# A two-row weight product, taken as raw fp32 instead of as a split pair, at the start of a fused diffusion block

## The chip, the cores and the metric

The kernel runs on one core of one Trainium2 chip. The metric is the device time of one execution in microseconds (us); the lower the better. TensorE (PE) multiplies, VectorE (DVE) and ScalarE (ACT) do elementwise work, GpSimd (POOL) does some of it too, and SyncE (SP) issues most DMA transfers.

## What is computed

One layer of a diffusion backbone over 512 latent tokens and 256 context tokens of width 1024, in fp32. The part that the change touches is the very first: two conditioning vectors, one for the latent tokens and one for the context tokens, go through a SiLU and are multiplied by the modulation weights; the first two of the six blocks of 1024 columns give the shift and the scale of the first normalisation.

```python
silu_c = jax.nn.silu(c)
silu_cc = jax.nn.silu(c_ctx)
mod = silu_c @ w_mod[i] + b_mod[i]
mod_c = silu_cc @ w_mod[i] + b_mod[i]
sh1, sc1, g1, sh2, sc2, g2 = jnp.split(mod, 6, axis=-1)
csh1, csc1, cg1, csh2, csc2, cg2 = jnp.split(mod_c, 6, axis=-1)
h = modulated_norm(x, g_norm1[i], sh1[:, None], sc1[:, None])
hc = modulated_norm(ctx, g_norm1[i], csh1, csc1)
proj = h @ w_in[i]
...
x = x + g1 * mix_stream(...)
x = x + g2 * moe(modulated_norm(x, g_norm2[i], sh2, sc2), ...)
return rmsnorm(x, g_final)
```

After it come the input projection, a bidirectional state-space scan (SSD) with its convolution, a pooling branch, a gated MLP branch, the merge with the output projection, and a mixture of 16 experts.

## The kernel before, in words

Nearly every large product is made of three: each fp32 operand is split into a high part `hi`, rounded to a reduced fp32 form (fp32r), and a rest `lo`, and TensorE multiplies high by high, high by low and low by high (`mm3`, lines 102 to 105). The weights are split as they arrive (`split`, lines 81 to 90): ACT writes `hi` (line 87), DVE or POOL writes `lo` as the difference (line 89).

The first phase (lines 764 to 866) computes shift and scale. Its weights are read as 16 tiles `wraw` of 128 x 1024 fp32 (512 KB), eight for each half `hf` of the columns: a tile holds 128 rows of the weights and 512 columns of the shift beside 512 of the scale. `w_unit` (line 798) loads one tile through a pool of five buffers, splits it, and multiplies `hi` and `lo` by `cs4`, four columns: the high and the low parts of the two conditioning vectors. Each half accumulates over its eight tiles into two PSUM tiles of 4 x 512 (`ptmp` for the first half, `pacc` for the second). A buffer comes free for the load five tiles later when the split has read it.

`rows_to_cols` (line 808) copies the four rows out (DVE line 810, ACT line 811), turns them into columns on TensorE while adding high and low rows with `sel4` (line 815), and makes `sh` and `gs` on DVE (lines 821 to 823). `h_block` (line 825) transposes the normalised tokens (line 830), applies `gs` and `sh` (line 835), and splits the result into `hTh` and `hTl` (lines 837, 838). The first half serves the blocks j = 0 to 3, the second half the blocks 4 to 7.

Behind it, `dt_phase` (line 887) multiplies a small slice of the input weights, turns it into columns (line 901), and runs a chain of small DVE operations (lines 905 to 920) which ends in products on TensorE (lines 924 to 926). `xbc_tile` and `conv_tile` make the inputs of the scan (convolution on DVE, line 970), `z_block` the gate (ACT, line 1168), `ssd_decay` and `ssd_group` the scan; `mix_prep` prepares constants for the later branches (lines 1030, 1032).

The order on each engine is set by a scheduler from the program text and its own costs. Engines take their instructions in that order, so an instruction that waits holds back all that stand behind it on its engine.

Of the kernel before, what the change touches and what calls it, by code (L numbers as in the profile page):

```python
# [7 lines left out]
FT = mybir.dt.float32  # L8
# [3 lines left out]
AF = mybir.ActivationFunctionType  # L12
# [7 lines left out]
KD = 8  # L20
# [18 lines left out]
def dap(t, off, ap):  # L39
    return bass.AP(tensor=t.tensor, offset=t.offset + off, ap=ap)  # L40
# [3 lines left out]
def backbone_kernel(ctx: ExitStack, tc: tile.TileContext, x, c, ctxt, c_ctx, w_mod, b_mod, g_norm1,  # L44
# [4 lines left out]
    V, S, G, T = nc.vector, nc.scalar, nc.gpsimd, nc.tensor  # L49
# [5 lines left out]
    def pool(name, bufs=1, space=None, side="left"):  # L55
        kw = {"space": space} if space else {"reuse_waits": "tile"}
        return tc.tile_pool(name=name, bufs=bufs, **({"side": side} if space is None else {}), **kw)
# [16 lines left out]
    def ptmp(shape=None, dt=FT):  # L74
        return tmp.tile(shape or [128, 512], dt, tag="tmp", name="ptmp")
# [5 lines left out]
    def split(raw, n, after=None):  # L81
        nsplit[0] += 1
        eng = G if lo_eng[0] is None and nsplit[0] % 1000 == 3 else lo_eng[0] or V
        hp_, lp_ = more_hl if more_hl and nsplit[0] % 4 == 0 else (hip, lop)
        hi = hp_.tile([128, 1024], FR, tag="hi", name="hi")
        lo = lp_.tile([128, 1024], FR, tag="lo", name="lo")
        S.activation(hi[:, :n], raw[:, :n], AF.Copy)  # L87
        with tc.issue_after(after.ins) if after else nullcontext():
            eng.tensor_tensor(lo[:, :n], raw[:, :n], hi[:, :n].bitcast(FT), op=OP.subtract)  # L89
        return hi, lo  # L90
# [668 lines left out]
    sck = sc.rearrange("p (q k) -> p k q", q=2)  # L759
    V.tensor_copy(cs4[:, :, 0:2], sck)  # L760
    V.tensor_tensor(cs4[:, :, 2:4], sck, cs4[:, :, 0:2].bitcast(FT), op=OP.subtract)
    sel4 = cst.tile([4, 2], FT)
    V.tensor_tensor(sel4, ident[0:4, 0:2], ident[0:4, 2:4], op=OP.add)
    with ExitStack() as p1:
        xp = p1.enter_context(pool("xp"))
        f1p = p1.enter_context(pool("f1p", 2))
# [7 lines left out]
        def load(dst, src):  # L774

            with tc.issue_after(queue[0].ins) if queue[0] else nullcontext():
                queue[0] = nc.sync.dma_start(dst, src)
# [20 lines left out]
        def w_unit(hf, k, pm):  # L798
            raw = wrp.tile([128, 1024], FT, tag="wraw", name="wraw")
            load(raw.rearrange("p (s n) -> p s n", s=2),  # L800
                 dap(w_mod, k * 128 * 6144 + hf * 512, [[6144, 128], [1024, 2], [1, 512]]))
            hi, lo = split(raw, 1024)
            for s in range(2):
                cs = slice(s * 512, (s + 1) * 512)
                T.matmul(pm[s], lhsT=cs4[:, k], rhs=hi[:, cs], start=k == 0, stop=False)
                T.matmul(pm[s], lhsT=cs4[:, k], rhs=lo[:, cs], start=False, stop=k == KD - 1)

        def rows_to_cols(hf, pm):
            mrow = f1p.tile([4, 2, 512], FT, tag="mrow", name="mrow")
            V.tensor_copy(mrow[:, 0], pm[0])  # L810
            S.activation(mrow[:, 1], pm[1], AF.Copy)
            pv = ptmp([128, 2, 4, 2])
            for s in range(2):
                for j in range(4):
                    T.matmul(pv[:, s, j], lhsT=mrow[:, s, j * 128:(j + 1) * 128], rhs=sel4, start=True, stop=True)
            js = slice(hf * 4, hf * 4 + 4)

            def bc(c0):
                return pcol[:, c0 + hf * 4:c0 + hf * 4 + 4].unsqueeze(2).to_broadcast([128, 4, 2])

            V.tensor_tensor(sh[:, js], pv[:, 0], bc(24), op=OP.add)
            V.tensor_tensor(gs[:, js], pv[:, 1], bsc1[:, js].unsqueeze(2).to_broadcast([128, 4, 2]), op=OP.add)
            V.tensor_tensor(gs[:, js], gs[:, js], bc(16), op=OP.mult)
# [18 lines left out]
        pm = [ptmp([4, 512]) for _ in range(2)]  # L842
        for k in range(KD):
            w_unit(0, k, pm)
            if k == 1:
                norm_x(2, 6)
        pm2 = [pacc([4, 512]) for _ in range(2)]
        w_unit(1, 0, pm2)
        w_unit(1, 1, pm2)
        rows_to_cols(0, pm)  # L850
        w_unit(1, 2, pm2)
        w_unit(1, 3, pm2)
# [3 lines left out]
        load_x(0)  # L856
        load_x(1)
        rows_to_cols(1, pm2)
        norm_x(0, 2)
        for j in range(4):  # L860
# [525 lines left out]
```

## Time and profile before

| | us |
|---|---|
| median of 3 runs (lowest, highest) | 1037.87 (1037.62, 1039.67) |
| the profiled execution, its own time | 1038.74 |
| its span, from the first to the last instruction | 1036.9 |
| PE busy in the span | 946.9 |
| DVE busy | 820.9 |
| ACT busy | 596.9 |
| POOL busy | 189.7 |

The rows further down are quoted from this one profiled execution. Times in them are microseconds from the start of the span; mean durations are in ns where marked. A matmul's end is modelled, so that successive products overlap in the rows.

### The profile page before, as it was taken

What the parts mean: (1) busy time and instruction counts of PE and PEld (TensorE: products, weight loads), DVE (VectorE), ACT (ScalarE), POOL (GpSimd) and SP (SyncE); (2) the same over time, 40 slices, a digit from 0 to 9 for tenths busy, and PEclk for the clock granted to TensorE, in tenths of its full rate; (3) what the DMA queues carried; (4) which work ended last, traced back from release to release, by engine and by line L of the source; (5) the groups of instructions that cost most, each with busy time, mean ns of one, the idle gap of its engine ahead of it and who ended that gap; (6) DMA issues with size and microseconds to landing.
All of it is one profiled execution on the core that took longest, in us unless ns stands there. A gap on an engine that the chain in (4) does not pass through costs nothing.

```text
span 1036.9 us, 13348 instructions
## 1 busy us (share of the span) xinstructions
PE 946.9 (91%) x4598; PEld 769.4 (74%) x4598; DVE 820.9 (79%) x1221; ACT 596.9 (58%) x884; POOL 189.7 (18%) x144
## 2 busy tenths in 40 slices
PE   3897989998898979999999999978999999999964
PEld 0486778886786857888888888867888888888842
DVE  6878976997878996677486434579999999999897
ACT  5665846667556333622332432445788888888843
POOL 2024313114222340000000010331111111111140
PEclk9998999999999989999999999988999999999987
DMA  8832361314223222276576558678999999999322
GB/s 271 280 91 60 119 201 41 116 47 143 61 61 86 64 65 71 82 244 215 172 217 210 162 166 288 257 245 318 326 355 362 361 375 372 375 361 364 107 73 82
DMA packets 100898, 203.92 MB, mean 197 GB/s; under 512 B 9998, under 2 KB 55290, under 8 KB 100827
## 3 DMA queue, kind: packets, MB, share of 16 engines
q1 hardware_dynamic: 95474, 194.19, 54.5%
q0 software_dynamic: 5136, 8.78, 3.6%
q8 instruction: 37, 0.61, 0.2%
q14 instruction: 35, 0.28, 0.1%
q10 hardware_dynamic: 216, 0.07, 0.0%
HBM read 197.25 MB, written 13.71 MB: 203 GB/s over the span
## 4 chain that ended last, share of the span: by engine, by line
PE 64%; DVE 22%; ACT 5%; DMA 4%; issue 3%; ACTq 0%; POOL 0%; SPq 0%; DVEq 0%; POOLq 0%
PE pacc L104 18%; PE pacc L103 18%; PE pacc L105 18%; DVE cv L970 5%; DVE lo L89 2%; PE ptmp L400 1%; DMA wraw<-in_w_mod_dram 1%; DVE w L1132 1%; DMA agb<-agd 1%; PE ptmp L1094 1%; PE ptmp L1096 1%; DVE agb L1126 1%; PE ptmp L423 1%; DVE r L1274 1%; DVE y L1103 1%
## 5 line engine op out<-in xcount | busy, mean ns | idle before, releaser
L87 ACT ACTIVATE hi<-raw 128x1024 fp32r<-128x1024 f32 (+1 forms) x199 | 209.0, 1057 | 168.0 <-PE pacc L104 75.9
L89 DVE TENSOR_TENSOR lo<-raw,hi 128x1024 fp32r<-128x1024 f32 (+1 forms) x165 | 203.6, 1254 | 58.8 <-ACT hi L87 51.7
L103 PE MATMUL pacc<-hTh,hi 128*128 128x512 f32 (+1 forms) x392 | 156.7, 401 | 4.9 <-ACT ytok L1168 3.5
L104 PE MATMUL pacc<-hTl,hi 128*128 128x512 f32 (+1 forms) x392 | 158.0, 403 | 0.0
L105 PE MATMUL pacc<-hTh,lo 128*128 128x512 f32 (+1 forms) x392 | 156.6, 400 | 0.0
L104 PE MATMUL pacc<-lo,xhl 128*128 128x512 f32 x384 | 151.5, 395 | 4.2 <-DVE lo L89 3.9
L103 PE MATMUL pacc<-hi,xhl 128*128 128x512 f32 x384 | 153.1, 402 | 0.0
L105 PE MATMUL pacc<-hi,xhl 128*128 128x512 f32 x384 | 150.5, 393 | 0.0
L89 POOL TENSOR_TENSOR lo<-raw,hi 128x1024 fp32r<-128x1024 f32 x34 | 91.1, 2684 | 197.6 <-ACT hi L87 187.8
L103 PEld LDWEIGHTS pacc<-hTh,hi 128*128 128x128 f32 (+1 forms) x392 | 74.0, 189 | 21.5 <-ACT ytok L1168 3.9
L104 PEld LDWEIGHTS pacc<-lo,xhl 128*128 128x128 f32 x384 | 72.9, 190 | 20.4 <-DVE lo L89 6.1
L970 DVE SCALAR_TENSOR_TENSOR cv<-xr,pcol,cv 128x770 f32<-128x770 f32 (+1 forms) x64 | 70.9, 1108 | 20.9 <-ACT cv L968 20.2
L105 PEld LDWEIGHTS pacc<-hTh,lo 128*128 128x128 f32 (+1 forms) x392 | 73.9, 189 | 16.2 <-issue 1.0
L104 PEld LDWEIGHTS pacc<-hTl,hi 128*128 128x128 f32 (+1 forms) x392 | 74.0, 189 | 16.0 <-issue 1.1
L105 PEld LDWEIGHTS pacc<-hi,xhl 128*128 128x128 f32 x384 | 72.5, 189 | 15.5
L103 PEld LDWEIGHTS pacc<-hi,xhl 128*128 128x128 f32 x384 | 72.9, 190 | 14.6
L142 DVE SCALAR_TENSOR_TENSOR lacc<-raw,sc,lacc 128x1024 f32<-128x1024 f32 x32 | 41.1, 1284 | 29.4 <-DMA raw<-in_w_mod_dram 29.0
L89 DVE TENSOR_TENSOR lo<-r,hi 128x1024 fp32r<-128x1024 f32 x42 | 50.1, 1219 | 4.7 <-PE pacc L104 3.0
L87 ACT ACTIVATE hi<-r 128x1024 fp32r<-128x1024 f32 x42 | 44.0, 1062 | 7.8 <-PE pacc L105 7.2
L480 POOL DMA_INDIRECT xg<-h2d,toki x16 | 19.2, 1201 | 156.8 <-PE ptmp L400 82.5
L1145 PE MATMUL pacc<-lo,hTh 128*128 128x512 f32 x96 | 38.6, 402 | 0.0
L1144 PE MATMUL pacc<-hi,hTh 128*128 128x512 f32 x96 | 38.2, 398 | 0.0
(410 smaller groups left out, 1894.8 us busy)
## 6 DMA issues: line engine op xcount, KB each, us to landing
raw<-in_w_e_in_dram SPq DMA_DIRECT2D x78, 512.0 KB
raw<-in_w_in_dram SPq DMA_DIRECT2D x60, 512.0 KB
raw<-in_w_e_out_dram SPq DMA_DIRECT2D x36, 512.0 KB
raw<-in_w_mod_dram SPq DMA_DIRECT2D x32, 512.0 KB
r<-in_w_e_in_dram SPq DMA_DIRECT2D x28, 512.0 KB
wraw<-in_w_mod_dram SPq DMA_DIRECT2D x16, 512.0 KB
agb<-agd SPq DMA_DIRECT2D x16, 512.0 KB
r<-in_w_e_out_dram SPq DMA_DIRECT2D x14, 512.0 KB
```

The costliest lines, as they stand in the source:

```text
L87: S.activation(hi[:, :n], raw[:, :n], AF.Copy)
L89: eng.tensor_tensor(lo[:, :n], raw[:, :n], hi[:, :n].bitcast(FT), op=OP.subtract)
L103: T.matmul(ps, lhsT=sh, rhs=mh, start=first, stop=False)
L104: T.matmul(ps, lhsT=sh, rhs=ml, start=False, stop=False)
L105: T.matmul(ps, lhsT=sl, rhs=mh, start=False, stop=last)
L142: V.scalar_tensor_tensor(a, raw, sc[:, k:k + 1], a, op0=OP.mult, op1=OP.add)
L400: T.transpose(pt[:, k], xgt[:, (h * 4 + k) * 128:(h * 4 + k + 1) * 128], ident)
L423: T.transpose(pt[:, k], hid[:, k * 128:(k + 1) * 128], ident)
L480: G.indirect_dma_start(out=dst, out_offset=None, in_=h2d[:, :], in_offset=bass.IndirectOffsetOnAxis(ap=idx, axis=0), bounds_check=L - 1, o ...
L970: V.scalar_tensor_tensor(oo, r[:, lo0 + j:lo0 + j + n], wcol(j), oo, op0=OP.mult, op1=OP.add)
L1144: T.matmul(pv[t], lhsT=a, rhs=wh[:, kk], start=k == 0, stop=False)
L1145: T.matmul(pv[t], lhsT=a, rhs=wl[:, kk], start=False, stop=False)
```

## The change

For the first half (`hf == 0`) the tile is no longer split. Its two 512-column parts are multiplied, as the fp32 values that were loaded, by `sck`, the two fp32 columns of the conditioning vectors. `rows_to_cols` then copies two rows instead of four and uses the first two rows of `sel4`, which are an identity. The second half stays as it was.

```diff
@@ w_unit
             load(raw.rearrange("p (s n) -> p s n", s=2),
                  dap(w_mod, k * 128 * 6144 + hf * 512, [[6144, 128], [1024, 2], [1, 512]]))
+            if hf == 0:
+                for s in range(2):
+                    T.matmul(pm[s][0:2], lhsT=sck[:, k], rhs=raw[:, s * 512:(s + 1) * 512],
+                             start=k == 0, stop=k == KD - 1)
+                return
             hi, lo = split(raw, 1024)
@@ rows_to_cols
-            mrow = f1p.tile([4, 2, 512], FT, tag="mrow", name="mrow")
-            V.tensor_copy(mrow[:, 0], pm[0])
-            S.activation(mrow[:, 1], pm[1], AF.Copy)
+            nr = 2 + hf * 2
+            mrow = f1p.tile([4, 2, 512], FT, tag="mrow", name="mrow")[:nr]
+            V.tensor_copy(mrow[:, 0], pm[0][:nr])
+            S.activation(mrow[:, 1], pm[1][:nr], AF.Copy)
...
-                    T.matmul(pv[:, s, j], lhsT=mrow[:, s, j * 128:(j + 1) * 128], rhs=sel4, start=True, stop=True)
+                    T.matmul(pv[:, s, j], lhsT=mrow[:, s, j * 128:(j + 1) * 128], rhs=sel4[:nr], start=True,
+                             stop=True)
```

Lines behind the insertion move down: line 805 of the kernel before is line 810 of the changed one, 815 is 821, 830 is 837, 1168 is 1175. The scheduler also writes the engines' orders anew, as far as the pooling branch; from there on they are the same.

On PE, the end of the first half and the start of the second, before (`sel` is `sel4`, `x` the tokens, `cs` is `cs4`):

```order
L805 MATMUL ptmp<-hi,cs_131 4x512 x2
L806 MATMUL ptmp<-lo,cs_131 4x512 x2
L815 MATMUL ptmp<-sel_134,mrow 128x2 x4
L830 MATMUL ptmp<-ident,x_147 128x128
L830 MATMUL ptmp<-ident,x_151 128x128
L830 MATMUL ptmp<-ident,x_155 128x128
L805 MATMUL pacc<-hi,cs_131 4x512 x2
```

The same place on PE in the changed kernel:

```order
L722 MATMUL ptmp<-ident,crow 128x80
L804 MATMUL ptmp<-wraw,sc 2x512 x16
L810 MATMUL pacc<-hi,cs_131 4x512 x2
L821 MATMUL ptmp<-sel_134,mrow 128x2 x4
L837 MATMUL ptmp<-ident,x_147 128x128
```

The 32 products of split tiles in the first half have become 16 of raw tiles, in one piece.

On SP, the queue of the loads, before (`x` of `in_ctx_dram` is a context token tile, `raw` a tile of the input weights, the first of them for `dt_phase`):

```order
L777 DMA wraw<-in_w_mod_dram 128x2x512 x7
L94 DMA raw<-in_w_in_dram 128x8x32
L777 DMA wraw<-in_w_mod_dram 128x2x512
L94 DMA raw<-in_w_in_dram 128x8x128
L777 DMA wraw<-in_w_mod_dram 128x2x512 x8
L777 DMA x_392<-in_ctx_dram 128x1024
```

The same place on SP in the changed kernel:

```order
L777 DMA wraw<-in_w_mod_dram 128x2x512 x16
L777 DMA x_344<-in_ctx_dram 128x1024
L777 DMA x_348<-in_ctx_dram 128x1024
L94 DMA raw<-in_w_in_dram 128x8x32
L94 DMA raw<-in_w_in_dram 128x8x128 x4
```

The two loads of input weights that stood among the `wraw` loads now stand behind all sixteen of them and behind the context tokens.

On ACT, where the first gate block is read out of PSUM (line 1168) amid the decay weights of the scan, before:

```order
L1168 ACT_TABLE_LOAD
L1168 ACTIVATE ytok<-pacc 128x512
L1125 ACTIVATE w<-agb,nag 128x128 x4
L1131 ACTIVATE w<-cbu,dtt 128x128 x2
L1128 ACT_TABLE_LOAD
L1128 ACTIVATE agb<-agb 128x512
L1168 ACT_TABLE_LOAD
L1168 ACTIVATE ytok<-pacc 128x512 x3
L1030 ACTIVATE wsT<-ptmp 128x512
```

The same place on ACT in the changed kernel:

```order
L1135 ACTIVATE agb<-agb 128x512
L1138 ACTIVATE w<-cbu,dtt 128x128 x2
L1175 ACT_TABLE_LOAD
L1175 ACTIVATE ytok<-pacc 128x512 x4
L1037 ACTIVATE wsT<-ptmp 128x512
```

Two of the three table loads ahead of `wsT` are gone from here; the whole program has 38 of them before and after.

## Rows read from the trace of the kernel before

**Rows 1.** The page: busy time by engine, and the longest chain by engine.

```profile
PE 946.9 (91%) x4598; PEld 769.4 (74%) x4598; DVE 820.9 (79%) x1221; ACT 596.9 (58%) x884; POOL 189.7 (18%) x144
...
PE 64%; DVE 22%; ACT 5%; DMA 4%; issue 3%; ACTq 0%; POOL 0%; SPq 0%; DVEq 0%; POOLq 0%
```

**Rows 2.** Chain of waits, 0 to 120 us: start, length, what ended last.

```profile
9.06 8.89 DMA wraw<-in_w_mod_dram
...
36.39 5.20 DMA wraw<-in_w_mod_dram
...
49.06 1.87 PE ptmp L815 x16
```

**Rows 3.** Timeline of PE, first half: start, length, what [idle before <- releaser].

```profile
15.31 1.01 PE L805 MATMUL ptmp<-hi,cs 128*4 128x512 f32 x2 [5.35 <-ACT hi L87]
...
19.17 1.00 PE L805 MATMUL ptmp<-hi,cs 128*4 128x512 f32 x2
21.78 0.63 PE L806 MATMUL ptmp<-lo,cs 128*4 128x512 f32 x2 [1.62 <-DVE lo L89]
...
28.75 0.62 PE L806 MATMUL ptmp<-lo,cs 128*4 128x512 f32 x2
```

**Rows 4.** Busy time by stretch; behind the engines: granted clock, DMA share, GB/s.

```profile
20.00:23.40 3.40, 1.37 (x5) 0.18 (x4) 2.78 (x3) 3.40 (x5) 0.00 (x0) 1.00 0.82 210
23.40:26.80 3.40, 3.18 (x8) 0.97 (x9) 3.40 (x4) 2.81 (x3) 0.00 (x0) 0.50 1.08 336
```

**Rows 5.** Instructions by tile, tile wraw: durations min/median/max in ns, starts.

```profile
L87 ACT ACTIVATE hi<-wraw x16: 1040/1042/1059, 14.2 to 41.7; 128x1024 fp32r<-128x1024 f32 x16
L89 DVE TENSOR_TENSOR lo<-wraw,hi x16: 1210/1218/1226, 15.3 to 44.8; 128x1024 fp32r<-128x1024 f32 x16
```

**Rows 6.** Timeline of PE, two raw fp32 products, then one, 512 columns each.

```profile
374.12 3.78 PE L1286 MATMUL ptmp<-o,pwt 128*128 128x512 f32 x4 [5.99 <-DVE o L1280]
...
391.42 1.13 PE L1286 MATMUL ptmp<-o,pwt 128*128 128x512 f32 x2 [1.43 <-DVE o L1280]
```

**Rows 7.** Busy time by stretch, at these two places (granted clock third from the end).

```profile
374.00:376.00 2.00, 1.88 (x3) 0.85 (x4) 2.00 (x2) 0.60 (x1) 2.00 (x1) 0.50 0.00 0
391.00:393.00 2.00, 1.35 (x3) 0.49 (x3) 2.00 (x3) 0.42 (x1) 0.00 (x0) 1.00 0.00 0
```

**Rows 8.** Timeline of SP, its DMA issues.

```profile
23.59 13.16 SPq L777 DMA_DIRECT2D wraw<-in_w_mod_dram  x8
```

**Rows 9.** Waits of the SP queue, 0 to 60 us: total, times, longest.

```profile
SPq L777 <- DVE lo L89: 15.6, 11, 2.9
```

**Rows 10.** Timeline of DVE, 29 to 50 us.

```profile
29.18 0.68 DVE L810 COPY mrow<-ptmp 4x512 f32<-4x512 f32 x1 [1.07 <-PE ptmp L806]
...
32.92 0.17 DVE L821 TENSOR_TENSOR sh<-ptmp,pcol 128x8 f32<-128x8 f32 x1 [0.96 <-PE ptmp L815]
...
34.42 0.80 DVE L835 TENSOR_SCALAR f<-ptmp,gs,sh 128x512 f32<-128x512 f32 x1
...
36.28 0.68 DVE L838 TENSOR_TENSOR hTl<-f,hTh 128x512 fp32r<-128x512 f32 x1
...
47.49 0.68 DVE L810 COPY mrow<-pacc 4x512 f32<-4x512 f32 x1 [0.56 <-PE pacc L806]
```

**Rows 11.** Waits of PE, 45 to 100 us: total, times, longest.

```profile
PE ptmp L924 <- DVE inv L1046: 5.4, 1, 5.4
```

**Rows 12.** Timeline of ACT, then of PE, at the first gate block.

```profile
129.50 1.28 ACT L1128 ACT_TABLE_LOAD   x1
...
132.03 1.28 ACT L1168 ACT_TABLE_LOAD   x1
...
135.44 1.13 PE L1032 MATMUL ptmp<-wsT,ones 128*128 128x512 f32 x2 [0.56 <-ACT wsT L1030]
```

**Rows 13.** Busy time by stretch, the scan and what follows the pooling branch.

```profile
92.00:360.00 268.00, 248.28 (x1286) 208.30 (x1286) 221.73 (x409) 161.76 (x310) 78.76 (x45) 0.98 0.32 95
...
400.00:660.00 260.00, 259.92 (x1186) 213.66 (x1184) 154.61 (x179) 93.28 (x130) 11.72 (x16) 1.00 0.61 198
```

## The prediction

> **What bounds the kernel now.** I read the page first: PE is busy for 91% of the span, and 64% of the longest chain runs through it [rows 1]. Then the busy times by stretch: between 400 and 660 us PE is busy 259.92 of 260 us [rows 13], and there its order is the same before and after. So whatever the change gains or loses up to the pooling branch is carried to the end, and the question is when PE gets through the first 400 us.
>
> The chain of waits shows what sets the pace at the start: the loads of the `wraw` tiles, first plainly (8.89 us), then again for the last tile, whose load is issued at 36.39 and ends 5.20 us later; after it come the products that turn the second half's rows into columns, at 49.06 [rows 2]. The loads are late because they wait for buffers: SP stood 15.6 us in all, eleven times, until DVE had written a `lo` [rows 9]. Five buffers stand against sixteen loads, and the first load of the second half was issued at 23.59 [rows 8]. The reader is to see here that the split holds the buffers. What the change gives PE in return, and whether the buffers come free earlier, is then the matter.
>
> **The cost of one raw product.** The timeline has raw fp32 products of 512 columns at another place: each shows as two records. Two products took 3.78 us at a granted clock of 0.50, one took 1.13 us at 1.00 [rows 6, 7]. With a record p long at full clock, 2p long at half, and a drain d: 8p + d = 3.78 and 2p + d = 1.13, so p = 0.44 and d = 0.25. [...] Those products had 128 weight columns and these have two. I take the same price: four weight columns in the first half and 128 elsewhere pay alike for fp32r products of 512 columns.
>
> **The first half.** Before, the first tile is there at 14.2, when its split starts [rows 5]; PE starts at 15.31 and ends at 28.75 + 0.62 = 29.4 [rows 3]. PE's work there is only 32 products; it waits for splits. In the changed kernel PE starts at 14.2 and has 8 x 1.77 = 14.1 us of work at full clock, 8 x 3.53 = 28.3 at half. The clock: pairs of products took 1.01 and 1.00 at the start and 0.63 from 21.78 [rows 3], so it ran at the half level until some 5 us after the first product; later a thin stretch (1.37 us busy of 3.40) was followed by one at 0.50 [rows 4]. I take 5 us at half, then full: 5 / 3.53 = 1.42 tiles, then 6.58 x 1.77 = 11.6, so the first half ends at 14.2 + 5 + 11.6 + 0.2 = 31.0, that is **+1.6**. Bounds: full throughout, 28.5 (-0.9); half throughout, 42.7 (+13.3).
>
> [...]
>
> The removed 8 splits (1.04 us each on ACT, 1.22 on DVE [rows 5]) cost nothing now that could be won directly: they lie beside the loads, and DVE has nothing else to do until the first half is done. Their gain is the buffers. With the clock as above, the fourth tile is done at 23.8, and the first load of the second half goes out at 24.0 against 23.59 [rows 8]: **no gain**, since PE now holds a buffer about as long as the split did.
>
> **The second half.** Now DVE sets the pace. Behind the copy of the rows (before at 29.18, in the change at 31.0) it has to do 0.65 + 8 `lo` at 1.17 (back to back) + 4 `f` at 0.72 + 3 `hTl` at 0.62 + 0.4 of small ones + a wait of 0.96 for the columns [rows 5, 10] = 16.1 us, so the last `lo` ends at 47.1 and the copy of the second half's rows starts near 47.7, against 47.49 [rows 10]. Before, DVE was as late, because it waited for loads between. The last load goes out when the third `lo` is written, 6.2 us behind the first half: 37.2 against 36.39 [rows 2], and lands at 42.4, before DVE wants it.
>
> Moved with it: the small load for `dt_phase` now stands behind the sixteen tiles and two context tiles, two of 1.6 us each (512 KB at 336 GB/s [rows 4]) and about 1 us of its own after the last of them, near 46.5; its first two products stand ahead of the columns' products on PE, so these start at 48 to 49.5, against 49.06 [rows 2]. **0 for the phase** (from -2.3 to +1.5, by the first half's end and this load). Ahead of line 901 PE then has five products of 512 columns more to do and seven of 256 fewer. A wide one costs about 0.22 us (an estimate: 260 us over 1186 products [rows 13]), a narrow one half: +0.3.
>
> **Behind it.** Ahead of line 924, for which PE waited 5.4 us [rows 11], the new order has 73 products of 512 columns where there were 82. If the DVE chain to line 924 is as long, that wait grows by 9 x 0.22 = 2.0 and the work comes later. From 92 to 360 us PE is idle for 19.7 of 268 us [rows 13], so other waits may cover it: 0 to +2.0, taken as **+1.0**. At the first gate block two table loads of 1.28 us leave the way to `wsT`, for which PE waited [rows 12]: -2.6 to 0 there; but they come back later on ACT: 0 to +2.6. Taken as **-1.3**. Other small moves in the scan I set at nothing, with their cover the same idle time.
>
> Sum: 0 + 0.3 + 1.0 - 1.3 = 0. The profiled execution took 1038.74, 0.87 above the median of the runs; against the median, I forecast **1037.9**, no change. A measurement of this kernel can tell about 0.2%, 2.1 us, from no change.
>
> **Rivals.**
>
> *Faster.* The clock rises early, the first half ends at 28.5, and DVE's 16.1 us start 2.5 us sooner than I take it, so that the copy starts at 45.2, 2.3 ahead of 47.49; the table loads at the gate are won and not paid again. For it: DVE and ACT are idle until the first half ends, and ACT waits often in the scan. Against it: the dt load still stands ahead of the columns' products. -2.3 - 2.6 + 0.3 + 0.5 = -4.1: 1033.8.
>
> *Slower, one mechanism: the clock stays at half* under raw products with two columns. The half ends at 42.7, DVE's work behind it begins 11.7 us later than in my sum, and no load is left to hide it: 1049.6. Each us at half beyond my 5 costs 0.5, so it decides once the clock stays down for some 9. Against it: with four columns the clock did rise [rows 3]; nothing in the trace shows two.
>
> *Slower, the order.* PE's 2.0 us behind line 924 aren't covered, and the table loads come back where ACT is waited for: 0.3 + 2.0 - 2.6 + 2.6 + 1.5 (late dt load) = +3.8: 1041.7.
>
> *The change doesn't do what it says:* raw tiles free buffers no sooner than split ones. That is my sum.
>
> **How the numbers follow.** No change 0.37 (1035.8 to 1040); faster rival 0.30; order rival 0.22; half clock 0.08; 0.03 for more gain in the scan than I can see. So faster 0.33, same 0.37, slower 0.30. The range takes in the ends of the two middle rivals with their bounds and leaves out the half clock: 1031.5 to 1043.5.
>
> **What would show it.** Right: 32 records on line 804, about 0.44 long at full clock; the last of them near 31; SP waiting for PE, not DVE, for loads 6 to 13; the copy of the second half's rows near 47.7; PE's wait at line 931 (924 before) longer than 5.4; one table load less ahead of the gate's rows. Wrong: a granted clock of 0.50 through the 20s; records of half that length; the columns of the second half more than 1.5 us from 49; or a scan whose end moves by more than 3 us against the end of the first phase.

## The result, and the profile after

The changed kernel takes 1045.69 us (median of 9 runs, 1040.98 to 1050.12) against 1037.87 (9 runs, 1035.34 to 1039.67): a ratio of 1.0076, interval 1.0055 to 1.0097. It is slower. The profiled execution took 1047.23 with a span of 1045.5, 8.6 more than the span of before.

The engines' shares hardly change [rows 1], and the first half does what it should. The page (busy time, and the longest chain by engine), then PE's busy time by stretch (granted clock third from the end), then the tile view (min/median/max in ns):

```profile
PE 958.2 (92%) x4598; PEld 774.5 (74%) x4598; DVE 808.3 (77%) x1213; ACT 589.5 (56%) x876; POOL 186.9 (18%) x144
...
PE 66%; DVE 21%; ACT 5%; DMA 4%; issue 2%; POOL 0%; ACTq 0%; SPq 0%; DVEq 0%; POOLq 0%
```

```profile
18.50:30.40 11.90, 11.90 (x29) 2.30 (x28) 0.88 (x2) 1.66 (x3) 0.00 (x0) 1.00 0.84 265
```

```profile
L804 PE MATMUL ptmp<-wraw,sc x32: 592/592/1057, 14.4 to 29.8; 128*2 128x512 f32 x32
```

The 32 records start at 14.42; from 18.6 on they follow each other every 0.43 us, before that every 0.85, and the last ends at 30.3. From 18.5 PE is busy without a gap (11.90 of 11.90 us) at a granted clock of 1.00. SP now waits for PE where it waited for DVE [rows 9], and the copy of the second half's rows starts where it did [rows 10]. SP's waits from 0 to 60 us (total, times, longest), then DVE's timeline:

```profile
SPq L777 <- PE ptmp L804: 12.9, 8, 3.7
SPq L777 <- DVE lo L89: 5.2, 3, 4.0
```

```profile
47.70 0.67 DVE L816 COPY mrow<-pacc 4x512 f32<-4x512 f32 x1
```

The loss begins behind it. PE's timeline before and after, from 43 us (start, length, [idle before <- releaser]); L815 and L821 are the columns, L103 to L105 with 512 columns are wide products of `dt_phase` and of the scan's first tile:

```profile
43.63 0.47 PE L103 MATMUL pacc<-hTh,hi 128*32 128x512 f32 x1 [1.37 <-ACT hi L87]
...
45.60 0.63 PE L104 MATMUL pacc<-hTl,hi 128*32 128x512 f32 x1
46.03 0.63 PE L103 MATMUL pacc<-hTh,hi 128*128 128x512 f32 x1
46.45 0.63 PE L104 MATMUL pacc<-hTl,hi 128*128 128x512 f32 x1
...
47.52 0.40 PE L105 MATMUL pacc<-hTh,lo 128*32 128x512 f32 x1
...
48.99 1.94 PE L815 MATMUL ptmp<-sel,mrow 4*128 4x2 f32 x16
```

```profile
44.13 0.62 PE L811 MATMUL pacc<-lo,cs 128*4 128x512 f32 x2 [1.37 <-DVE lo L89]
44.60 0.62 PE L810 MATMUL pacc<-hi,cs 128*4 128x512 f32 x2
46.88 1.02 PE L811 MATMUL pacc<-lo,cs 128*4 128x512 f32 x2 [1.66 <-DVE lo L89]
47.70 0.63 PE L103 MATMUL pacc<-hTh,hi 128*32 128x512 f32 x1
48.12 0.63 PE L104 MATMUL pacc<-hTl,hi 128*32 128x512 f32 x1
48.68 3.57 PE L821 MATMUL ptmp<-sel,mrow 4*128 4x2 f32 x16
```

Before, ten wide products stand ahead of the columns, in time that PE otherwise waits; after, two. Busy time by stretch, first before (from 52 to 60 it stayed at 1.00), then after, shows what became of the clock:

```profile
44.00:48.00 4.00, 4.00 (x13) 1.71 (x12) 3.44 (x6) 3.42 (x7) 0.00 (x0) 0.59 0.75 187
48.00:52.00 4.00, 4.00 (x28) 2.99 (x27) 2.40 (x7) 1.35 (x3) 0.00 (x0) 1.00 0.73 199
```

```profile
44.00:48.00 4.00, 2.21 (x7) 0.65 (x8) 3.62 (x7) 3.42 (x9) 0.00 (x0) 0.73 1.17 281
48.00:52.00 4.00, 4.00 (x18) 3.32 (x16) 0.76 (x3) 2.52 (x3) 0.00 (x0) 0.50 1.13 281
52.00:56.00 4.00, 4.00 (x13) 2.24 (x13) 3.67 (x11) 0.63 (x1) 0.00 (x0) 0.50 0.32 67
56.00:60.00 4.00, 4.00 (x22) 2.86 (x21) 1.52 (x3) 1.16 (x1) 0.00 (x0) 0.99 0.67 212
```

PE ran at half for 10.2 us, from 45.8 to 56.1. The columns took 3.57 instead of 1.94, and from their end to line 908 (901 before) PE took 20.9 instead of 18.6: line 908 starts at 73.11 against 69.55, **+3.56**. From there to the end of the scan another **+5.3** is added (285.4 against 280.1). By the four groups, each from the last `ytok` of one to that of the next, the first ends 1.5 us sooner after line 908, and the others take 4.3, 0.9 and 1.7 longer. Behind the scan nothing changes: PE's busy time is as before [rows 13].

```profile
92.00:360.00 268.00, 245.12 (x1256) 205.38 (x1257) 213.97 (x413) 159.02 (x307) 73.76 (x42) 0.96 0.32 93
400.00:660.00 260.00, 259.14 (x1168) 212.18 (x1169) 152.87 (x179) 91.31 (x124) 7.17 (x13) 1.00 0.58 186
```

### The profile page after: what moved, and what is told of

The parts are those of the page before. It is cut to its first block, busy times and chain, and to the rows that moved or that the text cites. A ratio compares the mean times of both kernels' runs of the same rounds, so it can differ in the third digit from the quotient of the medians.

```text
span 1045.5 us, 13314 instructions
## 1 busy us (share of the span) xinstructions
PE 958.2 (92%) x4598; PEld 774.5 (74%) x4598; DVE 808.3 (77%) x1213; ACT 589.5 (56%) x876; POOL 186.9 (18%) x144
## 4 chain that ended last, share of the span: by engine, by line
PE 66%; DVE 21%; ACT 5%; DMA 4%; issue 2%; POOL 0%; ACTq 0%; SPq 0%; DVEq 0%; POOLq 0%
PE pacc L104 18%; PE pacc L103 18%; PE pacc L105 18%; DVE cv L977 4%; DMA agb<-agd 2%; PE ptmp L804 2%; DVE lo L89 2%; PE ptmp L400 1%; DVE agb L1133 1%; DVE w L1139 1%; PE ptmp L1101 1%; PE ptmp L1103 1%; DVE w L1140 1%; PE ptmp L423 1%; DVE r L1281 1%
## 5 line engine op out<-in xcount | busy, mean ns | idle before, releaser
L103 PE MATMUL pacc<-hTh,hi 128*128 128x512 f32 (+1 forms) x392 | 160.0, 409 | 4.7 <-ACT ytok L1175 4.7
L105 PE MATMUL pacc<-hTh,lo 128*128 128x512 f32 (+1 forms) x392 | 158.9, 405 | 0.0
L103 PE MATMUL pacc<-hi,xhl 128*128 128x512 f32 x384 | 153.0, 401 | 0.0
L105 PE MATMUL pacc<-hi,xhl 128*128 128x512 f32 x384 | 151.3, 395 | 0.0
L89 POOL TENSOR_TENSOR lo<-raw,hi 128x1024 fp32r<-128x1024 f32 x34 | 88.4, 2602 | 206.7 <-ACT hi L87 206.6
L103 PEld LDWEIGHTS pacc<-hTh,hi 128*128 128x128 f32 (+1 forms) x392 | 75.0, 191 | 22.2 <-ACT ytok L1175 5.1
L105 PEld LDWEIGHTS pacc<-hTh,lo 128*128 128x128 f32 (+1 forms) x392 | 74.9, 191 | 16.1 <-issue 0.8
L105 PEld LDWEIGHTS pacc<-hi,xhl 128*128 128x128 f32 x384 | 72.8, 190 | 15.6 <-DVE xhl L402 0.2
L103 PEld LDWEIGHTS pacc<-hi,xhl 128*128 128x128 f32 x384 | 73.2, 191 | 14.5
L1132 ACT ACTIVATE w<-agb,nag 128x128 f32<-128x128 f32 x64 | 20.5, 392 | 37.3 <-PE ptmp L1103 28.1
```

The lines of the kernel that those rows point to most:

```text
L103: T.matmul(ps, lhsT=sh, rhs=mh, start=first, stop=False)
L105: T.matmul(ps, lhsT=sl, rhs=mh, start=False, stop=last)
L1132: S.activation(w[:, k], agb[:, 1, k], AF.Identity, bias=nag[:, t, b:b + 1])
```

## The experiments

All sixteen in one table, with the kernel before and the changed one. "Wide" is the number of wide products ahead of the second half's columns, "half" the time at the half clock between 44 and 60 us, "901" the start of line 901 (908), "scan" the end of the scan; these are from the one profile of each. One profile is one execution: the kernel before has its line 901 1.1 us apart in its two, the profiled execution of e4 took 1037.26 where the median was 1041.79, and that of e14 1047.07 where it was 1042.71. The ratio is to the kernel before, run again beside each, with its 95% interval; the last column is the range of the runs.

| kernel | wide | half | 901 | scan | ratio | runs |
|---|---|---|---|---|---|---|
| scan in about the order of before | | | | | | |
| before | 10 | 3.4 | 69.55 | 349.6 | | 1034.6 to 1043.0 (35) |
| e7 before again | 10 | 0 | 68.41 | 348.2 | one run | 1035.2 |
| e5 raw, loads earlier | 10 | 0 | 69.13 | 350.7 | 0.9984 [0.9969, 1.0000] | 1034.8 to 1039.4 |
| e10 split, loads earlier | 15 | 0 | 67.87 | 348.1 | 0.9983 [0.9970, 0.9995] | 1033.2 to 1038.1 |
| e11 three more tiles raw | 10 | 0 | 68.31 | 348.3 | 0.9989 [0.9976, 1.0003] | 1034.2 to 1039.5 |
| e12 four more tiles raw | 10 | 0 | 68.86 | 347.4 | 0.9995 [0.9983, 1.0007] | 1035.6 to 1040.0 |
| e9 raw, loads where before has them | 4 | 3.4 | 71.97 | 353.8 | 1.0029 [1.0017, 1.0041] | 1039.7 to 1043.4 |
| e3 raw, dt load in the middle | 2 | 3.4 | 71.80 | 353.4 | 1.0028 [1.0012, 1.0043] | 1038.4 to 1044.5 |
| e8 both halves raw, dt load as before | 1 | 0 | 71.17 | 354.2 | 1.0026 [1.0010, 1.0042] | 1039.0 to 1042.4 |
| scan in the order of the change | | | | | | |
| the changed kernel | 2 | 10.2 | 73.11 | 358.5 | 1.0076 [1.0055, 1.0097] | 1041.0 to 1050.1 |
| e6 the same again | 2 | 10.2 | 74.67 | 362.4 | 1.0086 [1.0054, 1.0117] | 1042.6 to 1052.6 |
| e15 agb load first | 2 | 10.2 | 73.46 | 359.0 | 1.0084 [1.0061, 1.0107] | 1042.1 to 1048.8 |
| e14 spare products, 35 to 39 us | 2 | 6.8 | 72.47 | 359.7 | 1.0042 [1.0021, 1.0063] | 1038.3 to 1052.5 |
| e2 spare products, 36 to 46 us | 2 | 6.8 | 72.78 | 355.5 | 1.0028 [1.0010, 1.0045] | 1037.0 to 1044.3 |
| e13 both kinds | 2 | 0 | 69.40 | 357.3 | 1.0024 [1.0003, 1.0045] | 1036.5 to 1047.5 |
| e16 e13, agb load first | 2 | 0 | 70.69 | 351.9 | 1.0035 [1.0016, 1.0055] | 1037.4 to 1047.5 |
| e4 both halves raw | 2 | 3.4 | 71.60 | 349.3 | 1.0038 [1.0017, 1.0059] | 1037.1 to 1048.9 |
| e1 split, dt load late | 2 | 13.7 | 73.89 | 353.8 | 1.0042 [1.0016, 1.0068] | 1035.9 to 1047.7 |

### First round: the late load, the clock, or the raw products?

**e1**, the kernel before with one load moved:

```diff
         load_x(1)
+        load(dtraw[:, :KD * 32].rearrange("p (k n) -> p k n", k=KD), cols(w_in, PW, 0, KD, OFF_DT, 32))
...
-            ph_, pl_ = unit(cols(w_in, PW, 0, KD, OFF_DT, 32), KD, 32)
+            h_, l_ = split(dtraw, KD * 32)
+            ph_, pl_ = (t_[:, :KD * 32].rearrange("p (k n) -> p k n", k=KD) for t_ in (h_, l_))
```

> The kernel before, with its split first half; only the small load for dt_phase is put behind all sixteen weight tiles and the two context tiles, where it stands in the changed kernel. The engines' order in the scan then comes out almost as in the changed kernel (66 DVE rows differ from before, 36 from the change). Theory A (the loss comes from the late load and the order behind it, not from the raw products): 1043 to 1048 us, line 901 at 72 to 74 us as in the changed kernel (73.1; before 69.6), the clock at half around 46 to 56. Rival R (the raw fp32 products themselves cost it): 1037 to 1039, line 901 near 69.6.

It is slower than before by 1.0042, without one raw product; line 901 at 73.89 and the clock at half from 44.0 to 57.6 are what theory A gave. The time is at its lower edge (1043.04), less than the changed kernel loses.

**e2**, spare products in the changed kernel's second half:

```diff
+        pdum = cxp.tile([128, 2, LC], FT, tag="cx", name="pdum").rearrange("p a b -> p (a b)")
...
+            if k >= 3:
+                T.matmul(pdum[0:2], lhsT=sck[:, k], rhs=raw[:, 0:512], start=True, stop=True)
             hi, lo = split(raw, 1024)
```

> The changed kernel with one raw fp32 product more for each of the last five tiles of the second half, written to a spare PSUM tile that nobody reads; the order of every engine is else the same row by row. Theory A1 (PE's idle stretches from 38 to 47 us let the clock fall to half for 45.8 to 56.1, and that alone moves the phase by 3.5): clock 1.00 through the 40s and 50s, the columns of the second half in 1.9 us instead of 3.5, line 908 at 69.5 to 70.5 instead of 73.1, the whole at 1041.5 to 1044 because what the scan adds (5.3) stays. Theory A2 (the order of the scan sets its own end and absorbs the phase): line 908 as in A1, but the end stays within 1.5 us of the changed kernel's 1045.7. Rival R: five products more, 1046 to 1050.

Five products more make it faster than the changed kernel: 1.0028, 1042.51 us, the time that A1 gave. Rival R falls. But the clock still fell, later and for 6.8 us; the columns took 2.3, and in this profile, of the slowest of its twelve runs, line 908 is only 0.3 us sooner than in the changed kernel. So the time came out as in A1 and the phase did not.

**e3**, the dt load behind the fourth tile of the second half (the load as in e1, at another place), and **e4**, no split in either half:

> The changed kernel with the small load for dt_phase put behind the fourth tile of the second half instead of behind all tiles and the context; its products can then fill PE from about 40 us, and the order of the scan comes out near that of before (142 PE rows differ, against 1321 for the changed kernel). Theory A: the clock stays up or falls for 3.4 us at most in the 40s, line 901 (908) at 69 to 70, the end at 1035 to 1039. Rival R: 1044 to 1048, for the raw products are all there.

```diff
-            if hf == 0:
-                for s in range(2):
-                    T.matmul(pm[s][0:2], lhsT=sck[:, k], rhs=raw[:, s * 512:(s + 1) * 512],
-                             start=k == 0, stop=k == KD - 1)
-                return
+            for s in range(2):
+                T.matmul(pm[s][0:2], lhsT=sck[:, k], rhs=raw[:, s * 512:(s + 1) * 512],
+                         start=k == 0, stop=k == KD - 1)
+            return
```

> Both halves are multiplied raw: no split of the modulation's weights at all; the loads and the scan's order stay nearly as in the changed kernel. Theory A: PE has 16 more products of 0.86 us and no gaps, the clock stays at 1.00 from 18.5 on, the second half ends at 44 to 45 instead of 47.9, line 908 at 66 to 69, the end at 1036 to 1042 (the scan's order still costs). Theory A2: 1044 to 1047. Rival R: twice the loss of the changed kernel, 1050 to 1056.

e3 is neither as before (theory A) nor as the change (R): line 908 at 71.8, 1.0028. The load was there, but the schedule still put two wide products ahead of the columns. That changed the theory: not when the load lands counts, but how many wide products PE does in its waits. In e4 the copy of the rows came at 47.74, not at 44 to 45, since PE itself was full; the time (1041.79) is not twice the loss, and R falls again.

### Second round: early loads

**e5**, the changed kernel with both loads early:

```diff
+            if k == 6:
+                load(raw0.rearrange("p (k n) -> p k n", k=KD), cols(w_in, PW, 0, KD, OFF_XBC + 8 * 128, 128))
+            if k == 4:
+                load(dtraw[:, :KD * 32].rearrange("p (k n) -> p k n", k=KD), cols(w_in, PW, 0, KD, OFF_DT, 32))
```

> The changed kernel with both early loads back where the kernel before has them: the small load for dt_phase behind the fifth tile, the first weights of the scan behind the seventh. The engines' order then is that of before but for the raw products (39 PE rows and 12 DVE rows differ), with ten wide products ahead of the second half's columns as before; the changed kernel has two. Theory A (late loads take the work out of PE's idle stretches, the clock falls, and the phase and the order behind it shift): line 901 (908) at 69 to 70.5 as before, the end within 2 us of before, ratio 0.997 to 1.002. Rival R (the raw products cost it): 1.005 to 1.010. If the buffers that the raw products free are worth anything once the loads stand right, it is below 0.998.

0.9984: the loss is gone, with every raw product in place. But the loads do not stand where the kernel before has them, though the expectation says so: there they come behind the seventh and the eighth tile, here behind the fifth and the seventh, and the small one is issued at 9.98 instead of 18.32:

```profile
9.98 0.89 SPq L777 DMA_DIRECT2D dtraw<-in_w_in_dram  x1
...
20.04 0.46 SPq L777 DMA_DIRECT2D raw<-in_w_in_dram  x1
```

PE's timeline has ten wide products ahead of the columns and no fall of the clock (1.00 from 44 to 60 us); the columns take 1.94 again:

```profile
44.09 0.42 PE L103 MATMUL pacc<-hTh,hi 128*32 128x512 f32 x1 [1.83 <-ACT hi L87]
...
46.41 0.39 PE L104 MATMUL pacc<-hTl,hi 128*128 128x512 f32 x1
...
48.58 1.94 PE L821 MATMUL ptmp<-sel,mrow 4*128 4x2 f32 x16
```

**e6** and **e7** are the changed kernel and the kernel before, with no edit.

> The changed kernel once more, nothing edited, beside the others on this chip, with a second profile. It tells which parts of its loss repeat. Expected under every theory: ratio 1.005 to 1.009. Theory A: line 908 at 72 to 74 again, the clock at half again from the mid 40s to the mid 50s. Theory S (the scan of a program in this order ends anywhere within some 6 us from run to run, by where half-clock stretches and table loads meet): from the columns of the second half to the end of the scan not the 306 us of the first profile, but 300 to 304; theory O (the order of the scan sets its length): 305 to 307 again.

> The kernel before once more, nothing edited, for a second profile: line 901 at 69.5 and the end of the scan at 349.6 in the first. Theory S: line 901 within 0.5 of 69.5, the end of the scan anywhere from 347 to 354. Theory O: the end of the scan within 1.5 us of 349.6.

The loss repeats (1.0086), and so do the half-clock stretch, from 47.5 to 57.7, and the late line 908. From the end of the columns to the end of the scan e6 takes 308.5 us and the first profile 306.3, the kernel before 298.4 and 298.7. That is nearer to theory O than to S, and in the kernel before O holds (348.2 against 349.6), though its line 901 came 1.1 us sooner than in its first profile, which S had within 0.5. But e2, in the same order as the changed kernel, had 304.5: the order alone does not set the length.

**e8**, e4 with the dt load behind the seventh tile, where the kernel before has it:

> Both halves raw, with the small load for dt_phase behind the seventh tile; the scan's order comes out near that of before (214 PE rows differ). PE is busy without a gap from 14 to 60 us, so that nothing can be filled in ahead of the columns, and DVE and ACT have no split of the modulation to do. Theory A: what is late is PE itself: line 901 at 71 to 72 as with both halves raw and the load late (71.6), ratio 1.000 to 1.004. If ACT and DVE being free counts: below 1.000. Rival R: 1.010 or more.

1.0026, line 908 at 71.17, as theory A had it: PE is full (16.00 of 16.00 us from 44 to 60), its columns end 2.1 us later than before, and nothing can be filled in. The clock stood at 1.00 in that stretch, so this loss is lateness without it.

### Third round: how many wide products

**e9** is e5 with the small load two tiles later (`k == 6`) and the scan's weights one tile later (`k == 7`), which is the order of loads in the kernel before; **e10** is the kernel before with the two loads where e5 has them.

> As the kernel with both loads early, but the two loads stand one and two tiles later: the small one behind the seventh tile, the scan's first weights behind the eighth. All raw products are there and both loads still land long before they are wanted; the scheduled order now puts only four wide products ahead of the second half's columns on PE instead of ten (98 PE rows differ from before, 39 there). Theory A, in its form after the first runs (what counts is how many of the wide products PE gets done in its idle stretches ahead of the columns): line 901 (908) at 70.5 to 72 instead of 69.1, ratio to before 1.000 to 1.004. Rival L (what counts is when the loads land): as with both loads early, line 908 near 69, ratio 0.997 to 1.000.

> The kernel before, split first half and all, with its two early loads two and one tiles earlier, behind the fifth and the seventh; fifteen wide products then stand ahead of the columns instead of ten (42 PE rows differ from before). Theory A: five wide products of 0.23 to 0.43 us less behind the columns, line 901 at 67.5 to 69 instead of 69.5 and 68.4, ratio 0.997 to 0.999, a gain without any raw product. Rival L: 0.999 to 1.001. If filling them in pushes the columns themselves back by as much, also 0.999 to 1.001, and the columns start at 50.

e9 is the cleanest pair with e5. Its loads are issued at 20.01 and 21.73 (18.32 and 22.17 in the kernel before), some 25 us before their products, yet it is slower by 0.0045 in the ratio. Its PE timeline has four wide products ahead of the columns; behind them the others run at half (0.63 long instead of 0.40):

```profile
46.28 0.39 PE L103 MATMUL pacc<-hTh,hi 128*32 128x512 f32 x1
...
48.91 1.94 PE L821 MATMUL ptmp<-sel,mrow 4*128 4x2 f32 x16 [0.63 <-DVE mrow L816]
...
52.16 0.63 PE L105 MATMUL pacc<-hTh,lo 128*32 128x512 f32 x1
52.59 0.63 PE L103 MATMUL pacc<-hTh,hi 128*32 128x512 f32 x1
```

Rival L falls. Line 908 is 2.8 us later than in e5. Of this the clock is only a part: six wide products that now stand behind the columns are some 1.4 us (an estimate, at 0.23 each as they follow each other in the rows), and the clock was at half for 3.4 us. The pair shows something else too: with the loads in their old order, the schedule of the raw kernel still puts four wide products ahead of the columns where that of the split one puts ten, and loses 0.0029. So the late loads are not the whole cause.

e10 gains 0.0017 without a raw product: line 901 is 1.7 us sooner than in the first profile of before, 0.5 sooner than in the second. With the loads at the same places, split (e10) and raw (e5) take the same time (0.9983 and 0.9984).

**e11** and **e12** take tiles of the second half raw too (e11: 1, 3, 5; e12: also 6), on top of e5:

```diff
+            if k in (1, 3, 5):
+                for s in range(2):
+                    T.matmul(pm[s][0:2], lhsT=sck[:, k], rhs=raw[:, s * 512:(s + 1) * 512],
+                             start=False, stop=False)
+                return
             hi, lo = split(raw, 1024)
```

> Both loads early, first half raw, and of the second half tiles 1, 3 and 5 raw too, into the first two of the four rows; DVE has three lo less (3.6 us) before it can copy the rows, and PE 5.2 us more in a stretch in which it waited. Theory: the copy of the second half's rows at 44 to 46 instead of 47.2 if DVE sets the pace there, line 901 at 67 to 68.5, ratio 0.994 to 0.998. If PE or the loads set the pace: the copy at 47, ratio 0.998 to 1.001.

> As the one before, with tile 6 raw as well: four lo less on DVE, 6.9 us more on PE. If DVE set the pace: the copy of the rows at 43.5 to 45.5, ratio 0.993 to 0.998; if PE becomes the bound, the copy no earlier than with three and the ratio higher than there by 0.001 or more.

The copy of the rows came at 46.5 and 46.2, only 0.7 and 1.0 us sooner than in e5, and the ratios are no better (0.9989, 0.9995). PE has become the bound; busy time from 31 to 48 us, e5 and e11:

```profile
31.00:48.00 17.00, 13.08 (x64) 5.72 (x63) 15.24 (x23) 12.55 (x19) 0.00 (x0) 1.00 0.85 266
```

```profile
31.00:48.00 17.00, 17.00 (x78) 7.30 (x78) 13.54 (x19) 11.13 (x17) 0.00 (x0) 1.00 0.91 292
```

### Fourth round: the rest of the loss

**e13** has the spare products of e2 and, behind the columns' products in the text, four more, which the schedule puts ahead of the last `lo` products; **e14** has only these four, and there the schedule puts them elsewhere.

```diff
                     T.matmul(pv[:, s, j], lhsT=mrow[:, s, j * 128:(j + 1) * 128], rhs=sel4[:nr], start=True,
                              stop=True)
+                    if hf == 1 and j % 2:
+                        T.matmul(pdum, lhsT=hTh[:, 0, 0:128], rhs=hTh[:, 0], start=True, stop=True)
```

> The changed kernel with the five spare raw products in the second half and four spare fp32r products of 128 columns by 512 more, which stand between the last lo product and the columns, where PE waits for the copy of the rows. Nothing else in any engine's order changes. Theory C (what the changed kernel loses beyond 3 us hangs on the clock's fall there): the clock falls for 3.4 us or not at all between 44 and 60, line 908 at 70.5 to 72, ratio 1.000 to 1.003. Rival D (the order of the scan makes it a matter of chance, and holding the clock did not give it back): 1.005 to 1.009.

> The changed kernel with the four spare fp32r products ahead of the columns alone, without the five raw ones: PE's gaps from 36 to 47 us stay as they are. Theory C: the clock falls near 46 as in the changed kernel, for 6.8 us or more, line 908 at 72.5 to 74.5, ratio 1.005 to 1.009. Rival D: any spare product in this stretch shifts the scan to a better phase, 1.001 to 1.004 as with the five.

e13, with nearly every other instruction in the changed kernel's order, keeps the clock. Its four products run where PE had waited 1.66 us for the last `lo`; then PE by stretch:

```profile
46.34 1.07 PE L826 MATMUL pdum<-hTh 128*128 128x512 f32 x4
```

```profile
44.00:48.00 4.00, 4.00 (x16) 1.49 (x14) 3.55 (x7) 2.89 (x8) 0.00 (x0) 1.00 1.20 273
48.00:52.00 4.00, 3.93 (x28) 2.97 (x27) 2.34 (x9) 2.50 (x3) 0.00 (x0) 1.00 1.04 265
52.00:56.00 4.00, 4.00 (x21) 2.70 (x20) 3.35 (x6) 1.79 (x2) 0.00 (x0) 1.00 0.69 169
```

Line 908 starts at 69.40, sooner than theory C gave and 3.7 us sooner than in the changed kernel, and the first three groups of the scan end 3.6, 3.8 and 3.7 sooner: the shift passes through. The ratio falls to 1.0024, with nine products more. e14 does not close the last gap: its four products run between the first split tiles, from 35.1 to 38.7, and PE's waits for `lo` stay, 4.2 us in four where the changed kernel has 4.4. In the tile view:

```profile
L824 PE MATMUL pdum<-hTh x4: 397/397/476, 35.1 to 38.7; 128*128 128x512 f32 x4
```

The clock falls at 48.2 for 6.8 us and line 908 is at 72.47, as theory C had it, but the ratio (1.0042) lies between the two theories: 0.0034 less than the changed kernel (the intervals overlap a little), with the waits much as they were. So not all that the ratio of e13 gives back can be put down to the waits that it closes.

In e13 the last group gave 2.5 of the 3.7 back. The chain showed a second wait for `agb` there, and SP's timeline a weight load between the last two loads of `agb`; before, these two stood together. The changed kernel's SP, then its chain, then SP of before:

```profile
327.06 0.34 SPq L1119 DMA_DIRECT2D agb<-agd  x1
333.03 0.37 SPq L94 DMA_DIRECT2D raw<-in_w_in_dram  x1
333.45 0.50 SPq L1119 DMA_DIRECT2D agb<-agd  x1
```

```profile
327.06 3.58 DMA agb<-agd
...
333.45 5.02 DMA agb<-agd
```

```profile
320.22 1.93 SPq L1112 DMA_DIRECT2D agb<-agd  x2
326.21 9.21 SPq L94 DMA_DIRECT2D raw<-in_w_in_dram  x2
```

**e15** and **e16** put that load behind the last `agb` load, in the changed kernel and in e13:

```diff
-            nc.sync.dma_start(agb.rearrange("p d k i -> p (d k i)"),
+            last_agb[0] = nc.sync.dma_start(agb.rearrange("p d k i -> p (d k i)"),
...
-        nc.sync.dma_start(raw[:, :k * n].rearrange("p (k n) -> p k n", k=k), ap)
+        n_wide[0] += k == 4
+        with tc.issue_after(last_agb[0].ins) if k == 4 and n_wide[0] == 5 else nullcontext():
+            nc.sync.dma_start(raw[:, :k * n].rearrange("p (k n) -> p k n", k=k), ap)
```

> The changed kernel with one load moved on the SP queue: the fifth weight load of 4 x 256 columns, which stands between the last two loads of agb, is issued behind them, as in the kernel before. All other engines keep their order. Theory Q (that queue position costs the last group its second wait): the last agb is issued within 2 us of the one before, the last group takes 58 to 60.5 us from end to end instead of 62.1 and 64.5, ratio 1.003 to 1.006. Rival D (chance of the scan, whatever the queue): ratio 1.007 to 1.009 and a last group of 62 or more.

> The same move in the kernel with nine spare products ahead of the second half's columns (clock held, line 908 at 69.4). Theory Q with the phase: both causes are gone, line 908 at 69 to 70, the last group at 58 to 60.5 instead of 64.5, ratio 0.997 to 1.001, and a spread of the runs of 6 us or less instead of 11. Rival D: 1.002 to 1.005 as without the move.

In the profiles the move does its local work: both loads go out within 1.9 us in e15 and 4.1 in e16, and the last group takes 60.7 and 58.1 us instead of 62.1 and 64.5. Nor is the move shown as the cause of that: e2, whose queue is that of the changed kernel, had a last group of 58.1 too. The ratios stay (1.0084, 1.0035). In e15 the third group took 70.0 instead of 68.3, with a half-clock stretch of 6.8 us at 278 where the changed kernel had 3.4; another of 6.8, at 322 (3.4 there), lies in the last group. As the cause of the rest theory Q falls.

## Why the prediction was wrong

**What held.** The price of a raw product (0.86 at full clock; the forecast's two records of 0.44 make 0.88, and four 1.77 for a tile, 3.53 at half, where the tiles before 18.6 took 3.4); the end of the first half (30.3; 31.0); SP waiting for PE for eight loads; the last load of the second half at 36.9 (37.2); the copy of its rows at 47.70 (47.7); the start of the columns at 48.7 (48 to 49.5). The start of the columns is what the forecast called the phase, so "0 for the phase" held. The gate lost its two table loads, and the first group ended 1.5 us sooner after line 908; how much of that is the gate's (1.3 forecast), and how much the shorter wait ahead of line 931, was not tried.

**The step that failed: from the columns to line 901, "+0.3".** Line 908 (901) came 3.56 us later, though the columns had started at 48.7 as forecast. The sum counted products and priced them at the full clock, and did not ask what PE would do while it waits for the second half's `lo`. Before, ten wide products lie there; after, two. The time at full clock was right: in e13, with the change's order and the clock held, line 908 is at 69.40 against 69.55, and from the end of the columns PE takes 19.0 against 18.6, the +0.3 of the forecast and 0.1 more. What was missing is the clock: 10.2 us at half cost 1.6 on the columns and 1.8 behind them (20.9 against 19.0). e5 against e9 shows in time what the fill is worth, the clock and the moved work together: with raw products and both loads early in both, ten or four wide products ahead go with 0.9984 and 1.0029.

The forecast had looked for a fall of the clock under the raw products of the first half, with half the clock throughout as its bound (42.7). The trace does not show it there. The records came at half their later pace until 18.6, for 4.2 us where the forecast took 5, and the granted clock was 1.00 from 18.5 to the end of the half at 30.3: a raw tile takes PE 1.72 us, and PE did not wait between tiles. The fall came in the second half, whose split tiles leave PE idle for up to 1.7 us each, and which the change robbed of its fill; from 45.8 the clock was at half. In this stretch the fall went with the wait; e4 has a fall without one (see the end). Of the forecast's own signs of an error one came true: the scan's end moved by 5.3 us against the end of the first phase.

**The second step: the scan, "+1.0", "-1.3" and the other moves "at nothing".** Together -0.3; measured, +5.3 from line 901 to the end of the scan. The wait ahead of line 931 became shorter, not longer: 3.8 us against 5.4 [rows 11], for line 931 came 19.6 us behind line 908 where 924 had come 21.8 behind 901:

```profile
PE ptmp L931 <- DVE inv L1054: 3.8, 1, 3.8
```

The gain of 1.5 by the end of the first group is there, but the next group takes 4.3 more. That is a move that the sum had at nothing. At the start of this group four table loads stand on ACT where two stood (at 166.01 and 172.89):

```profile
165.32 1.28 ACT L1135 ACT_TABLE_LOAD   x1
168.40 1.28 ACT L985 ACT_TABLE_LOAD   x1
172.70 1.28 ACT L1135 ACT_TABLE_LOAD   x1
174.65 1.28 ACT L980 ACT_TABLE_LOAD   x1
```

Table loads that come back are a part of the order rival, but its time, 1041.7, is 4.0 us short. The half-clock rival's, 1049.6, is as near from above; it had the clock, but under the raw products, where it did not fall. How much the loads are of the 4.3 was not tried.

**What is shown, and what stays open.** Some 3 to 4 us of the 8 are shown: kernels with too few wide products ahead of the columns lose about 3 us with a scan in the order of before (e3, e9), and holding the clock in the change's own order gives 3.7 back at line 908 in the profile, which last to the third group. In the ratio this is less clean, as e2 (1.0028) wins nearly as much as e13 while the clock still falls, and e14 (1.0042) more than half of it. The kernels in the change's order with the clock held still lose 0.0024 to 0.0035, and their runs spread over 10 to 11 us, against 3 to 6 in e3, e5 and e8 to e12. This part goes with the scan's new order; where in it was not settled.

The granted clock of each run says something on the rest. Its mean over the span has a median of 0.964 in the nine runs of the changed kernel, 0.959 to 0.963 in e6 and e15, against 0.969 in each of the five later sets of the kernel before; in e13 and e16 it is 0.968 and 0.970. 0.005 less of 1044 us is some 10 us more at half, up to 5 us of time (an estimate), where the fall at 45.8 cost 3.4. In the profiles, from 60 to 400 us, the changed kernel stands at half for 27 us and e6 and e15 for 34, the kernel before for 20 both times; e13, at 1044.44, for 34, e16, at 1038.57, for 24. So the loss beyond line 908 goes in good part with more falls of the clock in the scan; what brings them on was not tried, and why e1, with the longest fall at the start, loses only 0.0042 stays open.

No version beats the kernel before by much: e5 and e10 are 0.0016 and 0.0017 below it, and only the interval of e10 ends (just) below 1. Since e10 has no raw product, what little is gained comes from the loads' place.

## What to carry to other kernels

When a change makes a scheduler write an engine's order anew, count the instructions that the engine you depend on used to do in its waits, and ask what it has left: here the work that PE did in its waits cost nothing there (the columns start at 48.58 in e5 with ten wide products ahead, at 48.68 in the changed kernel with two), and with it the clock stayed at 1.00 (e5, e13), while the changed kernel, without it, had 10.2 us at 0.50. Compare kernels in nearly the same order, with one thing changed (here two explicit loads), before you judge such an edit, and look in the trace where an added instruction came to stand before you read its result. A wait removed from one place of a queue is won only if the median says so, not if one profile does (e15: a last group of 60.7 us instead of 62.1, and a ratio of 1.0084 against 1.0076).

## What the runs showed that was not expected

Under raw fp32 products with two weight columns the clock stood at 1.00 from 18.5 to their end at 30.3. In the first four us, from 14.4, the records came every 0.85 us instead of 0.43; the trace's own account of the clock begins at 18.5. In e4 the clock fell to half at 52.2, for 3.4 us, though PE had not waited since 18 us; just before, from 48.9 to 52.0, it did the sixteen columns' products, two columns each, four transposes and two wide products. That these brought on the fall is not shown: e8 has the same sixteen products from 49.5 to 53.1, PE as full, and the clock stayed at 1.00. PE's busy time in e4:

```profile
44.00:48.00 4.00, 4.00 (x14) 0.93 (x12) 2.91 (x7) 2.85 (x8) 0.00 (x0) 1.00 1.20 290
48.00:52.20 4.20, 4.20 (x27) 2.85 (x27) 2.50 (x7) 2.55 (x5) 0.00 (x0) 1.00 0.85 211
```

And the spread of a kernel's runs went with the order of its scan: 3 to 6 us over 11 or 12 runs each of seven kernels in the order of before (8.4 over 35 of the kernel before itself), 7 to 14 over 6 to 12 runs each of nine in the order of the change. In most kernels the longer runs had less granted clock: the changed kernel took 1040.98 at a mean of 0.967 and 1050.12 at 0.961, e13 1036.47 at 0.974 and 1047.46 at 0.964; in e8 the shortest and the longest, 1038.96 and 1042.41, both had 0.972.
